# Sums, squares and Toeplitz copies of a hybrid decoder step: from GpSimd to VectorE and ScalarE

## The chip, the cores and the metric

The kernel runs on the 8 cores of one Trainium2 chip, as two dies of four cores (0 to 3, 4 to 7). Each core has its own sequence and runs the same program, without traffic between cores. The metric is the device time of the slowest core in microseconds. Some executions are in a slow state, in which the cores of one die show a clearly lower granted clock; they are set aside, and only fast runs are compared.

Even among fast runs there is one more disturbance. In some of them the granted TensorE clock of some cores is 0.8125 for a stretch, mostly of some 150 us.

Engines: PE is TensorE, DVE is VectorE, ACT is ScalarE, POOL is GpSimd. In the lines of the profile ARENA stands for the kernel's buffers in SBUF, and PS for those in PSUM, into which the matmuls write (`PS<-ARENA`). An eviction is an instruction that takes a product out of PSUM. Excerpts of the profile show picked lines, word for word; lines between them are left out.

## The reference, cut to what matters

Four layers; every core takes one prompt of 2048 rows and 16 samples of 8 rows, in two passes of 1024 and 1152 rows. Weights are shared.

```python
for i in range(4):
    z = rmsnorm(h, g_mix) @ w_in            # three head groups: short conv, chunk mixing, Conformer conv
    h = h + concat(rmsnorm(y_a), rmsnorm(y_b), rmsnorm(y_c)) @ w_out
    f = rmsnorm(h, g_ffn)
    h = h + (silu(f @ w_gate) * (f @ w_up)) @ w_down          # the channel mixer, most of the work
    h = h + sigmoid(rmsnorm(h, g_ple) @ w_ple_gate) * (p[i] @ w_ple_proj)
y = rmsnorm(h, g_final)
```

## The kernel before

The kernel records operations in a graph, and a list scheduler written in Python plans them when the program is built: it assumes a duration for each operation and gives each to an engine. The orders and the waits between engines are then fixed. An operation lists the engines that may take it, with durations in ns; the first is the preferred one.

```python
def d_tt(n, psum=False, half=True):                  # tensor_tensor on VectorE
    if psum:
        return n / 0.96 + 64
    return n / (1.92 if half else 0.96) + 76
def d_pool(n):                                       # the same on GpSimd
    return 1.95 * n + 200

def tt(out_f, a_f, b_f, alu, n, r, w, psum=False, half=True, pool=True, ...):
    engs = {"dve": d_tt(n, psum, half)}
    if pool and not psum:
        engs["pool"] = d_pool(n)
    return g.op(engs, lambda e: e.tensor_tensor(out_f(), a_f(), b_f(), alu), r=r, w=w,
                lock=() if psum else LK, name=name, horizon=horizon)
```

The scheduler knows that GpSimd and VectorE's SBUF operations exclude each other, but only in its own time: nothing in the program enforces it.

```python
if e == "dve" and "dve" in o.lock and pool_lock[0] > t + 1e-9:
    k += 1          # VectorE takes no locked operation while GpSimd is planned to run
    continue
if e == "pool" and not o.dma and dve_lock[0] > t + 1e-9:
    k += 1
    continue
```

The channel mixer uses a Strassen form with seven products. Its operand sums are made on the fly, for the weights (1024 elements a partition, 1408 for the down projection) and for the activations (a quarter of the tile, 256 or 288 elements; 1024 or 1152 for the normed input).

```python
def sums(s):                                         # weight sums of one slab
    tt(sv(0), q(2), q(3), ALU.add, n, ...)
    tt(sv(1), sv(0), q(0), ALU.subtract, n, ...)
    tt(q(2), q(0), q(2), ALU.subtract, n, ...)
    tt(sv(2), q(1), sv(1), ALU.subtract, n, ...)
# activation sums behind SwiGLU: four tt of n = 2 * Q = 256 or 288
# squares of the norms: engs = {"act": d_act(n), "pool": d_pool(n), "dve": d_tt(n, False, not f32src)}
# ... the rest is cut
```

Evictions of the products are also `tt`, with one operand in PSUM; those go to VectorE alone.

## Time and profile before

| kernel before | value | where |
|---|---|---|
| fast runs | 3307.03, 3309.75, 3309.78 us | times |
| PE, DVE, ACT, POOL busy | 91%, 73%, 53%, 42% | page, part 1 |
| PE waiting for VectorE's tensor_tensor | 239.2 us, 51.4 of it the start | list of waits |
| 128x1024 f16 sum on VectorE | 972 ns on average, 685 ns where no GpSimd arithmetic overlaps it | groups by shape; records sorted by overlap |

From the page of the kernel before (core 2, one of those that had a stretch at 0.8125): the span, busy time of each engine, the chain of work that ended last (followed back from the last instruction, at each step to what released it), and the costliest groups (line, engine, operation, shapes, count; then busy us, mean ns of one; then idle time before them and who ended most of it).

```profile
span 3316.4 us, 62751 instructions; the slowest of 8 cores (3292.8 to 3316.4 us)
PE 3024.5 (91%) x23511; PEld 2236.6 (67%) x23542; DVE 2422.7 (73%) x4834; ACT 1752.5 (53%) x3392; POOL 1379.3 (42%) x1160
...
PE 69%; DVE 15%; ACT 6%; issue 5%; DMA 4%; SPq 0%; DVEq 0%; ACTq 0%
PE PS L933 69%; DVE ARENA L915 12%; ACT ARENA L908 3%; DVE ARENA L920 2%; DMA ARENA<-g 1%; DMA g<-ARENA 1%; ACT L764 1%; DMA ARENA<-x 1%; ACT ARENA L962 1%; ACT ARENA L974 1%; DVE ARENA L1302 0%; ACT ARENA L1531 0%; DVE ARENA L975 0%; DVE ARENA L1244 0%; DVE ARENA L1218 0%
...
L933 PE MATMUL PS<-ARENA 128*128 128x288 f16 (+7 forms) x23511 | 3024.5, 292 | 280.5 <-DVE ARENA L915 239.2
L915 POOL TENSOR_TENSOR ARENA<-ARENA 128x256 f16<-128x256 f16 (+11 forms) x811 | 1157.1, 1435 | 1099.4 <-DVE ARENA L915 700.2
L915 DVE TENSOR_TENSOR ARENA<-ARENA 128x1024 f16<-128x1024 f16 (+10 forms) x1889 | 1199.4, 674 | 124.6 <-ACT ARENA L962 54.1
L915 DVE TENSOR_TENSOR ARENA<-ARENA,PS 128x256 f32<-128x256 f32 (+9 forms) x2016 | 865.6, 446 | 553.3 <-PE PS L933 508.6
```

TensorE is the bottleneck: it is busy 91% and has 69% of the chain. GpSimd isn't in the chain at all. Yet the two lines for `tensor_tensor` on VectorE differ strangely: the one with SBUF operands alone has a mean of 674 ns, the one that reads PSUM 446 ns.

The list of waits (waiting engine and line, what it waited for; total us, times, longest us) says what stalls TensorE.

```profile
PE PS L933 <- DVE ARENA L915: 239.2, 160, 51.4
...
DVE ARENA L915 <- POOL ARENA L915: 7.5, 16, 0.6
```

TensorE waits for VectorE, and hardly anybody waits for a sum of GpSimd: VectorE does so for 7.5 us. The groups by shape, same columns as above, show how uneven VectorE's sums are.

```profile
L915 POOL TENSOR_TENSOR ARENA<-ARENA 128x1024 f16<-128x1024 f16 x134 | 299.8, 2243 | 193.6 <-DVE ARENA L915 190.2 <-ACT ARENA L908 1.2
L915 DVE TENSOR_TENSOR ARENA<-ARENA 128x1024 f16<-128x1024 f16 x274 | 258.8, 972 | 6.1 <-PE PS L933 4.9 <-ACT ARENA L1595 0.9
L915 DVE TENSOR_TENSOR ARENA<-ARENA 128x576 f16<-128x576 f16 x247 | 162.4, 696 | 14.7 <-ACT ARENA L908 14.2
L915 DVE TENSOR_TENSOR ARENA<-ARENA 128x256 f16<-128x256 f16 x188 | 98.2, 561 | 7.3 <-POOL ARENA L915 7.0 <-PE PS L933 0.3
L915 DVE TENSOR_TENSOR ARENA<-ARENA,PS 128x288 f32<-128x288 f32 x616 | 273.1, 450 | 215.5 <-PE PS L933 198.0 <-ACT ARENA L908 12.3
```

A sum of 256 elements takes 561 ns on average, longer than an eviction of 288 from PSUM (450 ns). The mean hides two populations, sorted here by whether a GpSimd arithmetic instruction overlaps: 128x1024 takes 685 ns (median) alone and 1257 ns (mean) overlapped, 128x576 452 and 1205 ns, 128x256 280 and 930 ns. Evictions from PSUM don't change (453 and 450 ns). (From here on, an instruction counts as blocked when work of GpSimd other than DMA issue overlaps it and it takes over 100 ns more than the median of its shape without overlap; what it takes more is the blocked time.)

The timeline around the entry to a channel mixer (start us, length us, engine, line, what, count, idle time before and what ended it):

```profile
2165.77 2.18 DVE L915 TENSOR_TENSOR ARENA<-ARENA 128x576 bf16<-128x576 bf16 x1
2168.96 5.43 DVE L915 TENSOR_TENSOR ARENA<-ARENA 128x576 f16<-128x576 f16 x2
2169.87 4.20 POOL L915 TENSOR_TENSOR ARENA<-ARENA 128x1024 f16<-128x1024 f16 x2
2174.32 0.81 DVE L915 TENSOR_TENSOR ARENA<-ARENA,PS 128x288 f32<-128x288 f32 x2
2174.54 0.56 PE L933 MATMUL PS<-ARENA 128*128 128x288 f16 x2 [3.29 <-DVE ARENA L915]
```

Two VectorE sums of 576 elements, some 0.9 us of work when nothing overlaps, take 5.43 us, while GpSimd works 4.20 us on two weight sums. The PSUM evictions that stand behind them in VectorE's order come at 2174.32, and TensorE, which waits for VectorE, has idled 3.29 us.

### The profile page before, as it was taken

The page shows a single profiled execution, that of the slowest core. Times are in us where ns is not written, and L with a number is a line of the kernel's source. Part 1 is how long each engine was busy: PE and PEld are TensorE (multiplying, and loading weights), DVE is VectorE, ACT ScalarE, POOL GpSimd, SP SyncE. Part 2 cuts the span into 40 slices and gives each one's busy share as a digit, 9 for nine tenths or more (in the row PEclk, how much of TensorE's full clock was granted, in tenths as well). Part 3 has the DMA queues.
Part 4 walks back from the last instruction along what each step waited for, and adds up shares of the span by engine and source line. Part 5 has one row for each costly group of instructions (what it writes and reads, how often), then busy time and mean ns, then how long its engine had stood idle before and what let it go on. Part 6 is the DMA issues. An engine that isn't in the chain of part 4 may idle for free.

```text
span 3316.4 us, 62751 instructions; the slowest of 8 cores (3292.8 to 3316.4 us)
## 1 busy us (share of the span) xinstructions
PE 3024.5 (91%) x23511; PEld 2236.6 (67%) x23542; DVE 2422.7 (73%) x4834; ACT 1752.5 (53%) x3392; POOL 1379.3 (42%) x1160
## 2 busy tenths in 40 slices
PE   3799998899989998899888999989999899998997
PEld 1468854787448854787556777667776677766776
DVE  2677586986778676985768767687676876858768
ACT  2654267444564367444585526855267552675525
POOL 0255533564346543565225343253432525415342
PEclk9888999999989999999989999999999999999999
DMA  6532465345623565447823346432465323643233
GB/s 127 117 64 49 81 111 107 72 78 101 138 50 57 96 108 109 77 81 149 180 51 65 60 86 131 85 64 57 75 130 101 60 52 75 132 97 62 52 73 94
DMA packets 87364, 294.90 MB, mean 89 GB/s; under 512 B 40224, under 2 KB 44576, under 8 KB 62496
## 3 DMA queue, kind: packets, MB, share of 16 engines
q0 software_dynamic: 31104, 222.18, 37.9%
q1 hardware_dynamic: 55968, 68.72, 7.1%
q8 instruction: 196, 3.21, 0.4%
q14 instruction: 96, 0.79, 0.1%
HBM read 481.71 MB, written 32.77 MB: 155 GB/s over the span
## 4 chain that ended last, share of the span: by engine, by line
PE 69%; DVE 15%; ACT 6%; issue 5%; DMA 4%; SPq 0%; DVEq 0%; ACTq 0%
PE PS L933 69%; DVE ARENA L915 12%; ACT ARENA L908 3%; DVE ARENA L920 2%; DMA ARENA<-g 1%; DMA g<-ARENA 1%; ACT L764 1%; DMA ARENA<-x 1%; ACT ARENA L962 1%; ACT ARENA L974 1%; DVE ARENA L1302 0%; ACT ARENA L1531 0%; DVE ARENA L975 0%; DVE ARENA L1244 0%; DVE ARENA L1218 0%
## 5 line engine op out<-in xcount | busy, mean ns | idle before, releaser
L933 PE MATMUL PS<-ARENA 128*128 128x288 f16 (+7 forms) x23511 | 3024.5, 292 | 280.5 <-DVE ARENA L915 239.2
L933 PEld LDWEIGHTS PS<-ARENA 128*128 128x128 f16 (+2 forms) x23542 | 2236.6, 99 | 1067.9 <-issue 390.9
L915 POOL TENSOR_TENSOR ARENA<-ARENA 128x256 f16<-128x256 f16 (+11 forms) x811 | 1157.1, 1435 | 1099.4 <-DVE ARENA L915 700.2
L915 DVE TENSOR_TENSOR ARENA<-ARENA 128x1024 f16<-128x1024 f16 (+10 forms) x1889 | 1199.4, 674 | 124.6 <-ACT ARENA L962 54.1
L915 DVE TENSOR_TENSOR ARENA<-ARENA,PS 128x256 f32<-128x256 f32 (+9 forms) x2016 | 865.6, 446 | 553.3 <-PE PS L933 508.6
L908 ACT ACTIVATE ARENA<-PS 128x256 f32<-128x256 f32 (+5 forms) x1756 | 715.1, 419 | 824.8 <-PE PS L933 703.5
L962 ACT ACTIVATE ARENA<-ARENA 128x512 bf16<-128x512 f32 (+3 forms) x415 | 267.7, 656 | 576.2 <-DVE ARENA L915 527.6
L908 ACT ACTIVATE ARENA<-ARENA 128x768 f16<-128x768 f32 (+6 forms) x284 | 238.4, 849 | 56.8 <-DVE ARENA L915 49.8
L974 ACT ACTIVATE ARENA<-ARENA 128x512 f16<-128x512 f32 (+3 forms) x356 | 255.3, 739 | 17.4 <-PE PS L933 12.5
L896 POOL DMA_DIRECT2D ARENA<-wpair x152 | 88.4, 582 | 404.4 <-PE PS L933 193.5
L764 ACT ACT_TABLE_LOAD x139 | 178.3, 1283 | 2.2
L920 DVE SCALAR_TENSOR_TENSOR ARENA<-ARENA,PS 128x288 f32<-128x288 f16 (+1 forms) x192 | 95.7, 526 | 29.9 <-PE PS L933 14.5
L908 ACT ACTIVATE ARENA<-PS,ARENA 128x288 f16<-128x288 f32 (+3 forms) x174 | 88.5, 561 | 31.6 <-PE PS L933 30.6
L1403 POOL TENSOR_TENSOR ARENA<-ARENA 128x3 f32<-128x3 f32 (+1 forms) x24 | 21.7, 904 | 143.0 <-DVE ARENA L1401 143.0
L975 DVE TENSOR_SCALAR ARENA<-ARENA 128x576 f16<-128x576 f16 (+3 forms) x156 | 71.8, 480 | 1.6 <-PE PS L933 0.3
L963 DVE TENSOR_TENSOR ARENA<-ARENA 128x576 bf16<-128x576 f16 (+3 forms) x93 | 50.0, 549 | 29.3 <-ACT ARENA L908 25.8
L963 POOL TENSOR_TENSOR ARENA<-ARENA 128x512 bf16<-128x512 f32 (+2 forms) x36 | 42.0, 1166 | 60.9 <-DVE ARENA L915 52.1
L1302 DVE SCALAR_TENSOR_TENSOR ARENA<-ARENA,PS 128x288 f16<-128x288 f16 (+3 forms) x56 | 38.4, 695 | 30.0 <-PE PS L933 29.6
L920 DVE SCALAR_TENSOR_TENSOR ARENA<-PS,ARENA 128x512 f16<-128x512 f32 (+2 forms) x96 | 48.4, 547 | 14.9 <-PE PS L933 14.4
L1595 ACT ACTIVATE ARENA<-ARENA 128x128 f16<-128x128 f16 (+1 forms) x66 | 43.8, 734 | 13.1 <-DVE ARENA L915 12.6
L896 POOL DMA_DIRECT2D ARENA<-wdn x32 | 18.8, 588 | 74.7 <-PE PS L933 54.3
L1218 DVE TENSOR_TENSOR ARENA<-ARENA 128x640 f16<-128x640 f32 x52 | 45.5, 932 | 0.0
(38 smaller groups left out, 257.3 us busy)
## 6 DMA issues: line engine op xcount, KB each, us to landing
ARENA<-wpair POOLq DMA_DIRECT2D x152, 1024.0 KB, 9.4
ARENA<-wdn POOLq DMA_DIRECT2D x32, 1408.0 KB, 11.5
t<-ARENA SPq DMA_DIRECT2D x4, 2560.0 KB, 16.5
ARENA<-t SPq DMA_DIRECT2D x4, 2560.0 KB, 16.9
ARENA<-wv POOLq DMA_DIRECT2D x8, 768.0 KB, 15.8
ARENA<-x SPq DMA_DIRECT2D x16, 288.0 KB, 13.6
y<-ARENA SPq DMA_DIRECT2D x16, 288.0 KB, 2.3
ARENA<-x SPq DMA_DIRECT2D x16, 256.0 KB, 28.8
```

Of the source, the lines that this page charges most:

```text
L764: e.preload_act_table_set(tbl[i])
L896: return g.op({"pool": 900}, lambda e: e.dma_start(out=out_f(), in_=in_f()), r=r, w=w, dma=nb, name=name, horizon=horizon)
L908: return e.activation(out_f(), in_f(), func, scale=scale if isinstance(scale, float) else scale(), **kw)
L915: return g.op(engs, lambda e: e.tensor_tensor(out_f(), a_f(), b_f(), alu), r=r, w=w, lock=() if psum else LK, name=name, horizon=horizon)
L920: return e.scalar_tensor_tensor(out_f(), a_f(), s_f if isinstance(s_f, float) else s_f(), b_f(), op0, op1)
L933: lambda e: e.matmul(out_f(), l_f(), r_f(), start=start, stop=stop, skip_group_check=True),
L962: return e.activation(sq.ap(), a, AF.Square)
L963: return e.tensor_tensor(sq.ap(), a, a, ALU.mult)
L974: return e.activation(hg.ap(), a, AF.Identity, scale=vc(gcol(k)))
L975: return e.tensor_scalar(hg.ap(), a, vc(gcol(k)), None, ALU.mult)
L1218: return e.tensor_tensor(o, a, b, ALU.mult)
L1595: lambda e, t=t, k=k, i0=i0, o0=o0, m=m: (e.activation(t.ap()[:, o0:o0 + m], x.ap()[:, i0:i0 + m], AF.Identity, scale=vc(V0 + 32 + k * 3 + j))
```

## The change

The intent is to take GpSimd's arithmetic away where VectorE or ScalarE can do it. In the built programs, GpSimd loses 859 `tensor_tensor`, VectorE goes from 4836 to 5724 instructions, and ScalarE from 3258 to 3230. GpSimd keeps DMA issue, memsets, tiny copies, eight mask products and the powers. The plan is made anew, so the order of everything else moves too.

```diff
--- before.py
+++ after.py
@@ -803,6 +803,7 @@
 
 PRODS = (1, 2, 6, 5, 7, 3, 4)
 PDT = F16
+POOL_MAX = 0
 
 
 def d_tt(n, psum=False, half=True):
@@ -910,7 +911,7 @@
 
     def tt(out_f, a_f, b_f, alu, n, r, w, psum=False, half=True, pool=True, name="tt", urgent=False, horizon=None):
         engs = {"dve": d_tt(n, psum, half)}
-        if pool and not psum:
+        if pool and not psum and d_pool(n) < POOL_MAX:
             engs["pool"] = d_pool(n)
         return g.op(engs, lambda e: e.tensor_tensor(out_f(), a_f(), b_f(), alu), r=r, w=w,
                     lock=() if psum else LK, name=name, horizon=horizon)
@@ -954,7 +955,7 @@
         hgs = {}
         for i, k in enumerate(ks):
             sq = g.tile([n], BF16, "sq", top=True)
-            engs = {"act": d_act(n), "pool": d_pool(n), "dve": d_tt(n, False, not f32src)}
+            engs = {"act": d_act(n), "dve": d_tt(n, False, not f32src)}
 
             def fsq(e, sq=sq, k=k):
                 a = src(k)()
@@ -1216,7 +1217,7 @@
                     a = CST.ap()[:, 0:16].unsqueeze(1).unsqueeze(3).to_broadcast([128, 5, 16, 8])
                     b = TV.ap()[:, 5 * q:5 * q + 5, :].unsqueeze(2).to_broadcast([128, 5, 16, 8])
                     return e.tensor_tensor(o, a, b, ALU.mult)
-                g.op({"dve": d_tt(640, False, False), "pool": d_pool(640)}, ftz, r=[(CST, 0), (TV, 0)], w=[(TZ, q)], lock=LK, name="tz")
+                g.op({"dve": d_tt(640, False, False)}, ftz, r=[(CST, 0), (TV, 0)], w=[(TZ, q)], lock=LK, name="tz")
             hw_dma(lambda: sct[l], lambda: flat(TZ), [(TZ, range(16))], [(dtz, 0)], 128 * 20480, name="tzst")
         else:
             hw_dma(lambda: flat(TZ), lambda: sct[l], [(dtz, 0)], [(TZ, range(16))], 128 * 20480, name="tzld")
@@ -1530,7 +1531,7 @@
                         if hasattr(e, "activation"):
                             return e.activation(tv(sq), cv(j), AF.Square)
                         return e.tensor_tensor(tv(sq), cv(j), cv(j), ALU.mult)
-                    g.op({"act": d_act(nn), "dve": d_tt(nn), "pool": d_pool(nn)}, fsq, r=[(CC[j], u)], w=[(sq, 0)], lock=LK, name="lsq")
+                    g.op({"act": d_act(nn), "dve": d_tt(nn)}, fsq, r=[(CC[j], u)], w=[(sq, 0)], lock=LK, name="lsq")
 
                 def p2():
                     rb = g.tile([nn], F16, "lrb", top=True)
```

## The prediction

> What bounds the kernel now. The page of core 2 (span 3316.4 us, granted clock 0.965) has PE busy 91%, DVE 73%, ACT 53%, POOL 42%. In the chain of waits PE has 69% and DVE 15%; POOL has none. By the groups PE idles 280 us, and DVE line 915 ends 239 us of it (51 us of that is the start). TensorE bounds the kernel; what can be won is the some 190 us in which it waits for VectorE, plus the half-clock stretches after such gaps.
>
> Why VectorE is late. The same instruction has two lengths. Grouping DVE records by shape and by whether a POOL arithmetic instruction overlaps: 128x1024 f16 sums take 685 ns alone, 1257 ns on average when overlapped; 128x576 f16 452 and 1205; 128x256 f16 280 and 930. Sums with a PSUM operand don't change (128x288: 453 and 450). The Trainium skill (SBUF — State Buffer, "Who interferes with whom") says that a DVE instruction with two SBUF inputs and a GpSimd instruction that reads SBUF exclude each other, the second blocking fully; this trace agrees. Over all shapes DVE loses 370 us so. In the timeline at 2169 us two 128x576 sums on DVE take 5.43 us while POOL runs two 128x1024 sums (4.20 us), and PE then idles 3.29 us.
>
> What the change moves. The instruction order of both built programs: POOL loses 859 tensor_tensor; DVE goes from 4836 to 5724, ACT from 3258 to 3230. Removed: about 1120 us of POOL work. Added to DVE, at unblocked medians (134 x 685 ns, 56 x 884, 164 x 280, 132 x 301, about 170 x 453, about 160 x 420 and so on): about 420 us. Removed from DVE: 370 us of blocking. So DVE busy should stay nearly level, 2400 to 2500 us: what POOL did costs VectorE about what it already paid for it.
>
> How much is on the critical path. Walking back from each PE gap ended by DVE through the unbroken run of DVE work before it: of 194 us of such gaps, 104 us follow runs with blocking in them. Per layer the entry to the channel mixer (580-640 us, 2160-2220 us) has about 12 us of PE gaps, some 17 us of blocking, 35 us of POOL work that becomes about 12 us of DVE work: a net relief of 5 to 7 us. Times eight layers, 40 to 55 us. The Trainium skill (TensorE: Matmul & The Clock Gate, Part 1) says an idle PE falls to half clock; the clock records agree (3.4 to 6.8 us at 0.5 after the gaps at 592, 603 and 2176 us), so 10 to 20 us more. Gaps ended by ACT-bound norms, the conv's DMA round trips and the start stay.
>
> Predicted 3240 us (2.1% faster), 3195 to 3285; chances 0.52 faster, 0.46 within 2%, 0.02 slower.
>
> Signs. Right: 128x1024 f16 sums on DVE all near 685 ns; DVE busy about 2450 us; POOL under 200 us; PE idle down from 280 us by 50 or more; the gap at the mixer's entry down from 3.3 us to about 1. Wrong: DVE busy above 2600 us; PE idle unchanged with DVE at 95% at the same stages.
>
> What would make it wrong. The plan is rebuilt and may put sums before PSUM evictions, which opens new gaps; the gaps may be bound by norm chains on ACT, then the gain is under 1%; a denser PE may be granted less clock.

## More of the kernel before

Where experiments are compared closely I use the profiled run and take the mean span over the cores whose clock record has no stretch at 0.8125 ("undisturbed cores"). That is cores 4 to 7 for the kernel before (3296.4 us) and all eight for the kernel after (3114.8 us).

## The result, and the profile after

In the rounds of the first comparison the fast runs of the changed kernel took 3124.08 and 3127.17 us, those of before 3307.03, 3309.75 and 3309.78. The ratio is 0.9446, with a 95% interval from 0.9419 to 0.9474; a ratio is the mean time of one kernel's fast runs over that of the other's in the same rounds. So it is 5.5% faster.

The page of the kernel after (core 3; L916 and L934 are L915 and L933 moved by the added line):

```profile
span 3122.5 us, 62461 instructions; the slowest of 8 cores (3108.2 to 3122.5 us)
PE 2959.3 (95%) x23542; PEld 2224.7 (71%) x23542; DVE 2399.4 (77%) x5722; ACT 1730.0 (55%) x3364; POOL 161.1 (5%) x301
...
PE 87%; ACT 4%; DVE 4%; DMA 4%; issue 1%; SPq 0%; DVEq 0%; POOL 0%; ACTq 0%
PE PS L934 87%; ACT ARENA L909 2%; DVE ARENA L916 2%; DMA ARENA<-x 1%; DVE ARENA L921 1%; DMA ARENA<-g 1%; ACT L764 1%; ACT ARENA L963 1%; DMA g<-ARENA 1%; DMA y<-ARENA 0%; DVE ARENA L1219 0%; SPq L894 0%; DVE ARENA L1303 0%; ACT ARENA L1532 0%; ACT ARENA L975 0%
...
L934 PE MATMUL PS<-ARENA 128*128 128x288 f16 (+6 forms) x23542 | 2959.3, 289 | 151.7 <-DVE ARENA L916 132.1
L916 DVE TENSOR_TENSOR ARENA<-ARENA 128x1024 f16<-128x1024 f16 (+11 forms) x2700 | 1232.6, 489 | 123.4 <-ACT ARENA L963 61.2
L916 DVE TENSOR_TENSOR ARENA<-ARENA,PS 128x256 f32<-128x256 f32 (+9 forms) x2016 | 867.1, 445 | 412.5 <-PE PS L934 399.0
```

From its list of waits:

```profile
PE PS L934 <- DVE ARENA L916: 132.1, 52, 53.4
```

GpSimd's busy share falls from 42% to 5%, and VectorE's busy time falls too, from 2422.7 to 2399.4 us, although it has 888 instructions more. TensorE's idle time in the group falls from 280.5 to 151.7 us; its wait for VectorE from 239.2 to 132.1 us, of which 53.4 us is the start.

The groups by shape of the kernel after:

```profile
L916 DVE TENSOR_TENSOR ARENA<-ARENA 128x1024 f16<-128x1024 f16 x408 | 272.7, 683 | 8.1 <-PE PS L934 6.7 <-ACT ARENA L1596 0.9
L916 DVE TENSOR_TENSOR ARENA<-ARENA 128x576 f16<-128x576 f16 x320 | 133.2, 451 | 6.2 <-ACT ARENA L909 4.3 <-PE PS L934 0.9
L916 DVE TENSOR_TENSOR ARENA<-ARENA 128x256 f16<-128x256 f16 x352 | 88.5, 285 | 2.3
L916 DVE TENSOR_TENSOR ARENA<-ARENA,PS 128x288 f32<-128x288 f32 x616 | 276.7, 450 | 163.5 <-PE PS L934 159.1 <-ACT ARENA L909 0.3
```

The means are now the unblocked times: 683 ns for a sum of 1024, 285 ns for 256. On undisturbed cores VectorE's busy time less its blocked time rose by some 345 us, while its blocked time fell by 373: the moved work costs VectorE a little less than it used to lose.

The timeline at the same stage of the kernel after; the matmul that ended the 3.29 us gap stands at 14794 in its trace, where the records of 31 earlier matmuls are missing, and number 14825 of the complete trace here starts at 2039 us. First TensorE's line, then VectorE's:

```profile
2009.82 50.36 PE L934 MATMUL PS<-ARENA 128*128 128x288 f16 x408
...
2031.59 0.44 DVE L916 TENSOR_TENSOR ARENA<-ARENA,PS 128x288 f32<-128x288 f32 x1
2031.95 0.81 DVE L916 TENSOR_TENSOR ARENA<-ARENA 128x576 f16<-128x576 f16 x2
2032.69 0.44 DVE L916 TENSOR_TENSOR ARENA<-ARENA,PS 128x288 f32<-128x288 f32 x1
2033.05 0.81 DVE L916 TENSOR_TENSOR ARENA<-ARENA 128x576 f16<-128x576 f16 x2
2033.79 0.44 DVE L916 TENSOR_TENSOR ARENA<-ARENA,PS 128x288 f32<-128x288 f32 x1
```

TensorE runs 50.36 us there without a break. VectorE alternates short sums and evictions. The busy time in a stretch of 60 us at that stage, before and then after:

```profile
core 2: us, PE busy (x) PEld busy (x) DVE busy (x) ACT busy (x) POOL busy (x), PEclk, DMA share, GB/s
2160.00:2220.00 60.00, 50.37 (x382) 36.57 (x381) 54.52 (x94) 29.36 (x60) 33.52 (x24) 0.97 0.38 71
```

```profile
core 3: us, PE busy (x) PEld busy (x) DVE busy (x) ACT busy (x) POOL busy (x), PEclk, DMA share, GB/s
2010.00:2070.00 60.00, 59.94 (x490) 47.62 (x489) 58.08 (x141) 42.02 (x79) 1.58 (x3) 1.00 0.40 77
```

VectorE's busy share went up, from 54.52 to 58.08 of 60 us, and TensorE's from 50.37 to 59.94. But the two stretches don't hold the same work: TensorE ran 382 matmuls in the first and 490 in the second. For the same matmuls VectorE is busy less long than before; a table in the section on the prediction has the figures.

Where 181.6 us went (3296.4 to 3114.8, mean of undisturbed cores, from the traces):

| part of TensorE's time | before | after | gain |
|---|---|---|---|
| idle between matmuls | 230.1 | 96.9 | 133.2 |
| lost to half clock while it works | 56.7 | 32.7 | 24.0 |
| the rest of its working time | 2946.3 | 2921.5 | 24.8 |

The three gains sum to 182.0; the start and the end took 0.4 us more. The second row is half of the time that the clock record has at 0.5, outside the idle gaps. The third row is mostly the other part of the same stalls. The profile models the end of a matmul: for 288 columns it stands 286 ns after the start (median), while the next matmul mostly starts after 123 ns. So where TensorE stalls, the last matmul still counts as busy for a while. Outside half clock, 210 matmuls a core were followed by an idle gap before and 70 after; beyond the gap itself their successors were 34.6 and 11.8 us late in all, which is 22.8 of the 24.8 us.

### The profile page after: what moved, and what is told of

Same layout as the page of the kernel before. It is cut to its first block, busy times and chain, and to the rows that moved or that the text cites. A ratio compares the mean times of both kernels' runs of the same rounds, so it can differ in the third digit from the quotient of the medians.

```text
span 3122.5 us, 62461 instructions; the slowest of 8 cores (3108.2 to 3122.5 us)
## 1 busy us (share of the span) xinstructions
PE 2959.3 (95%) x23542; PEld 2224.7 (71%) x23542; DVE 2399.4 (77%) x5722; ACT 1730.0 (55%) x3364; POOL 161.1 (5%) x301
## 4 chain that ended last, share of the span: by engine, by line
PE 87%; ACT 4%; DVE 4%; DMA 4%; issue 1%; SPq 0%; DVEq 0%; POOL 0%; ACTq 0%
PE PS L934 87%; ACT ARENA L909 2%; DVE ARENA L916 2%; DMA ARENA<-x 1%; DVE ARENA L921 1%; DMA ARENA<-g 1%; ACT L764 1%; ACT ARENA L963 1%; DMA g<-ARENA 1%; DMA y<-ARENA 0%; DVE ARENA L1219 0%; SPq L894 0%; DVE ARENA L1303 0%; ACT ARENA L1532 0%; ACT ARENA L975 0%
## 5 line engine op out<-in xcount | busy, mean ns | idle before, releaser
L934 PE MATMUL PS<-ARENA 128*128 128x288 f16 (+6 forms) x23542 | 2959.3, 289 | 151.7 <-DVE ARENA L916 132.1
L934 PEld LDWEIGHTS PS<-ARENA 128*128 128x128 f16 (+2 forms) x23542 | 2224.7, 99 | 886.0 <-issue 217.8
L916 DVE TENSOR_TENSOR ARENA<-ARENA 128x1024 f16<-128x1024 f16 (+11 forms) x2700 | 1232.6, 489 | 123.4 <-ACT ARENA L963 61.2
L916 DVE TENSOR_TENSOR ARENA<-ARENA,PS 128x256 f32<-128x256 f32 (+9 forms) x2016 | 867.1, 445 | 412.5 <-PE PS L934 399.0
L963 ACT ACTIVATE ARENA<-ARENA 128x512 bf16<-128x512 f32 (+3 forms) x398 | 257.5, 655 | 539.4 <-DVE ARENA L916 484.3
L975 ACT ACTIVATE ARENA<-ARENA 128x512 f16<-128x512 f32 (+3 forms) x341 | 247.1, 741 | 5.8 <-DVE ARENA L916 4.5
L897 POOL DMA_DIRECT2D ARENA<-wpair x152 | 81.6, 539 | 1993.8 <-PE PS L934 1114.3
L964 DVE TENSOR_TENSOR ARENA<-ARENA 128x576 bf16<-128x576 f16 (+3 forms) x146 | 81.1, 563 | 21.6 <-ACT ARENA L909 20.7
L909 ACT ACTIVATE ARENA<-PS,ARENA 128x288 f16<-128x288 f32 (+2 forms) x174 | 89.3, 561 | 10.4 <-PE PS L934 6.6
L976 DVE TENSOR_SCALAR ARENA<-ARENA 128x512 f16<-128x512 f16 (+3 forms) x171 | 67.4, 415 | 1.5 <-PE PS L934 0.2
L1408 DVE TENSOR_SCALAR ARENA<-ARENA 128x384 f16<-128x384 f32 x68 | 29.4, 475 | 8.6 <-POOL ARENA L1404 7.0
```

The lines of the kernel that those rows point to most:

```text
L897: return g.op({"pool": 900}, lambda e: e.dma_start(out=out_f(), in_=in_f()), r=r, w=w, dma=nb, name=name, horizon=horizon)
L909: return e.activation(out_f(), in_f(), func, scale=scale if isinstance(scale, float) else scale(), **kw)
L934: lambda e: e.matmul(out_f(), l_f(), r_f(), start=start, stop=stop, skip_group_check=True),
L963: return e.activation(sq.ap(), a, AF.Square)
L964: return e.tensor_tensor(sq.ap(), a, a, ALU.mult)
L975: return e.activation(hg.ap(), a, AF.Identity, scale=vc(gcol(k)))
```

## The experiments

Three theories were set against each other. BLOCKING: GpSimd's reads lock VectorE's two-input sums out. SLOW RESULT: the sums take two to three times as long on GpSimd, and something waits for them. REPLAN: without GpSimd the planner finds a better order, whatever the hardware does. Later a question was added: does lost VectorE time count, or the length of a single stall?

All figures in this section without another label are mean spans of undisturbed cores.

### The plan of before, executed by VectorE

```diff
+    moved = [i for i in g.orders["pool"] if g.ops[i].prim != "pool" and not g.ops[i].dma and g.ops[i].name not in ("wm", "wms")]
+    for i in moved:
+        g.ops[i].eng = "dve"
+    gone = set(moved)
+    g.orders["pool"] = [i for i in g.orders["pool"] if i not in gone]
+    g.orders["dve"] = sorted(g.orders["dve"] + moved, key=lambda i: (g.ops[i].start, i))
```

> The plan of before is made as it was, GpSimd included; afterwards the 859 tensor_tensor that it gave to GpSimd are executed by VectorE, at the place in VectorE's order that their planned start gives. Same order, same allocation, no work on GpSimd. Theory BLOCKING (GpSimd's reads lock VectorE out and that makes TensorE wait) and theory SLOW RESULT (the sums take 2 to 3 times as long on GpSimd and something waits for them): most of the gain is there, 3120 to 3170 us, TensorE idle under 180 us. Theory REPLAN (with GpSimd gone the planner finds a better order): little of the gain, 3250 to 3310 us.

Ratio to before 0.952 (0.944 to 0.960); 3157.8 us on undisturbed cores. TensorE's idle time between matmuls is 125.0 us, against 230.1 in before. So 138.6 of the 181.6 us come with before's own plan, in which only the engine differs. The other 43.0 us come with the new plan. REPLAN alone is out, but it isn't nothing.

### The plan and engines of before, with instructions on GpSimd that read nothing

```diff
-        return g.op(engs, lambda e: e.tensor_tensor(out_f(), a_f(), b_f(), alu), ...)
+        return g.op(engs, lambda e: e.memset(out_f(), 0.01) if ON[0] == "pool" else e.tensor_tensor(...), ...)
```

(The squares got the same edit. The result is wrong on purpose.)

> Plan, order and engines of before, but every sum and square that GpSimd did is a memset of the same output on GpSimd (result wrong on purpose). It reads nothing, so two-input sums on VectorE should not be blocked, and it is probably shorter. BLOCKING or SLOW RESULT: 3110 to 3180 us. REPLAN: 3250 us or more, as the plan is before's.

Ratio 0.950 (0.945 to 0.954); 3145.6 us. By shape:

```profile
L917 POOL MEMSET ARENA<- 128x1024 f16 x134 | 126.7, 955 | 216.7 <-DVE ARENA L917 209.4 <-ACT ARENA L910 5.8
L917 DVE TENSOR_TENSOR ARENA<-ARENA 128x1024 f16<-128x1024 f16 x274 | 180.0, 684 | 6.1 <-PE PS L935 4.7 <-ACT ARENA L1599 1.1
```

The plan is before's and GpSimd still does each of these steps, in 955 ns instead of 2243 for 1024 elements. VectorE's sums are at 684 ns. This run alone doesn't part BLOCKING from SLOW RESULT, since memset is also shorter. Together with the last one it prices the added work: the same plan with the moved sums on VectorE has 294.6 us more VectorE busy time (2396.1 against 2101.5) and is 12.2 us longer, 0.04 us of total for a microsecond. (The memsets can cost something themselves, as a later run shows, so this price is rather low.)

### Sums that nobody uses, put back on GpSimd

To the kernel after, whose plan stays the same to the instruction, 946 sums were added on a private tile, one every 3.15 us of planned time.

```diff
+                if not isinstance(i, int):
+                    e.wait_ge(sems[self.eidx["dve"]], i.count)
+                    ins = e.tensor_tensor(JUNK[:, 0:512], JUNK[:, 512:1024], JUNK[:, 512:1024], ALU.add)
+                    ins._wait_ge(semj, nj)
+                    ins.then_inc(semj, 1)
```

(The rest of the edit is cut. `i` is then a filler that stands between GpSimd's own instructions, and the first wait paces it by VectorE's progress.)

> The kernel after, plan unchanged to the instruction, plus 946 tensor_tensor 128x512 f16 on GpSimd (about 1.14 us each, 1.08 ms in all) on a private tile that nobody uses, each let go by a VectorE semaphore so that they spread evenly. BLOCKING: VectorE's two-input sums get long again (128x1024 f16 mean well over 800 ns instead of 685), total 3170 to 3290 us. SLOW RESULT and REPLAN: nobody waits for these sums and the plan is the good one, so 3115 to 3140 us.

The twin has `e.memset(JUNK[:, 0:1024], 0.0)` in place of the sum:

> As junk_read, but each junk instruction is a GpSimd memset of 128x1024 f16, which writes and reads nothing. All theories: 3115 to 3140 us, VectorE's two-input sums at 685 ns. If it is as slow as junk_read, then GpSimd being busy at all costs (semaphores, DMA issue behind it), not its reads of SBUF.

The sums cost everything the change had won: ratio to before 1.013 (1.006 to 1.019), 3352.2 us, which is even above the range of BLOCKING. The memsets: ratio 0.948 (0.942 to 0.953), 3143.1 us. The groups by shape, first of the run with sums, then of the one with memsets:

```profile
L776 POOL TENSOR_TENSOR JUNK<-JUNK 128x512 f16<-128x512 f16 x946 | 1095.6, 1158 | 1947.7 <-DVE ARENA L935 1619.4 <-DVE ARENA L940 92.2 <-DVE ARENA L983 66.0
L935 DVE TENSOR_TENSOR ARENA<-ARENA 128x1024 f16<-128x1024 f16 x408 | 319.0, 796 | 5.6 <-PE PS L953 4.9
L935 DVE TENSOR_TENSOR ARENA<-ARENA 128x576 f16<-128x576 f16 x320 | 168.5, 560 | 2.1 <-ACT ARENA L928 1.1
L935 DVE TENSOR_TENSOR ARENA<-ARENA 128x256 f16<-128x256 f16 x352 | 139.8, 429 | 2.3
```

```profile
L776 POOL MEMSET JUNK<- 128x1024 f16 x946 | 908.0, 960 | 1929.2 <-DVE ARENA L935 1608.5 <-DVE ARENA L940 85.1 <-DVE ARENA L983 72.4
L935 DVE TENSOR_TENSOR ARENA<-ARENA 128x1024 f16<-128x1024 f16 x408 | 272.7, 683 | 7.2 <-PE PS L953 6.7
L935 DVE TENSOR_TENSOR ARENA<-ARENA 128x576 f16<-128x576 f16 x320 | 133.2, 450 | 5.7 <-ACT ARENA L928 4.1 <-PE PS L953 0.4
L935 DVE TENSOR_TENSOR ARENA<-ARENA 128x256 f16<-128x256 f16 x352 | 88.6, 285 | 2.3
```

GpSimd's arithmetic is busy 1.14 ms with the sums and 0.96 ms with the memsets (1.26 ms in before). With sums, VectorE's 128x256 sums go from 285 to 429 ns on average and VectorE loses 423 us; with memsets they stay at 285 ns. Nobody waits for this result and the plan is the good one, so this is BLOCKING, and it is shown: what harms is that GpSimd reads SBUF while VectorE wants two SBUF inputs. SLOW RESULT isn't needed for a loss of this size; in before itself it isn't isolated by a run, but there only 7.5 us of VectorE's waits were for a sum of GpSimd. The memsets still cost 28 us over the kernel after, more than any theory here expected. In their run VectorE loses 64 us, among others in its 128x1024 tensor_scalar, which takes 476 ns alone and 1031 ns overlapped. That part would fit the Trainium skill (SBUF — State Buffer, "Who interferes with whom"): a VectorE instruction in a two-port mode contends with any GpSimd instruction, a two-input one only with those that read. Whether these tensor_scalar ran in such a mode isn't shown by the profile.

### Lost VectorE time, or the length of a stall?

The same pace, but the fillers stand in VectorE's own order, right after the instruction that paced them.

```diff
+                if name == "dve" and i in paced:
+                    ins = e.tensor_tensor(JUNK[:, 0:768], JUNK[:, 768:1536], JUNK[:, 768:1536], ALU.add)
```

(The rest of the edit is cut.)

> The kernel after, plan unchanged to the instruction, plus 946 tensor_tensor 128x768 f16 on VectorE itself (550 ns each alone, some 470 ns back to back, so about 440 us in all), on a private tile that nobody uses, at the same even pace as the junk of junk_read. VectorE so loses as much time as the 425 us that GpSimd's reads took from it in junk_read, which cost 240 us. LOST TIME (what counts is how much VectorE time goes, in whatever pieces; my prediction's sum rested on this when it set added work against removed blocking): about as slow as junk_read, 3290 to 3370 us. LONG STALL (what counts is that one urgent instruction is held for 1 to 2 us; pieces of half a microsecond are absorbed): 3130 to 3200 us.

3271.2 us (ratio 0.986, 0.983 to 0.989), with 383.8 us more VectorE busy time than the kernel after: 156.4 us of total, 0.41 us for a microsecond. It falls below the range of LOST TIME and far above that of LONG STALL. Short pieces that ignore urgency do hurt.

Then GpSimd fillers of other lengths, the edit being the shape (1024 every 6.3 us, 256 every 1.78 us):

> As junk_read (the kernel after, same plan, unused sums on GpSimd at an even pace), but 476 sums of 128x1024 f16 (2.13 us each) in place of 946 of 128x512: GpSimd is as long busy, about 1.05 ms, in pieces of double length. So far a blocked microsecond cost 0.5 us of total in before (370 blocked, 180 lost) and 0.55 in junk_read (425 blocked, 235 lost), 0.8 in pool_big (240 blocked, 190 lost). LONG STALL: 0.7 us or more per blocked microsecond, total 3360 us or more. LOST TIME: 0.5 to 0.6 as in junk_read, whatever the length.

> As junk_long, but 1594 sums of 128x256 f16 (about 0.67 us each), again about 1.05 ms in all. LONG STALL: 0.4 us or less per blocked microsecond, total 3180 to 3270 us. LOST TIME: 0.5 to 0.6 per blocked microsecond.

| fillers on GpSimd | VectorE blocked, us | mean block, us | total over the kernel after, us | per blocked us |
|---|---|---|---|---|
| 1594 of 256 | 249.3 | 0.34 | 113.3 | 0.45 |
| 946 of 512 | 423.3 | 0.61 | 237.4 | 0.56 |
| 476 of 1024 | 503.6 | 1.31 | 309.0 | 0.61 |

(Total: span less 3114.8 us. The last row is of cores 2 and 3 alone, as the others had a stretch at 0.8125; its ratio to before, 1.047, includes those; that of the first row is 0.977, 0.971 to 0.983. The total of the middle row holds what GpSimd's fillers cost without reading: against its twin with memsets it is 209.1 us, for 359 us more of lost VectorE time, 0.58 for one.) Neither theory passes its own test cleanly: 0.61 isn't 0.7, and 0.45 isn't 0.5 to 0.6. The cost per blocked microsecond grows mildly with the length. What grows more is the blocked time itself, which doubles from short to long fillers, though GpSimd's arithmetic is busy no longer (1.19 ms with the short ones, 1.02 ms with the long).

### Which of the moved sums did the harm

The new parameter lets one part go back. First the small ones, the activation sums (`POOL_MAX = 800`; 287 of 256 or 288 elements. The text calls them "Toeplitz-like"; they are Strassen operand sums):

> The change, but sums of up to 288 elements (155 of 256 and 132 of 288: the Toeplitz-like T sums behind the channel mixer's activations, about 0.7 us each, 200 us in all) may still go to GpSimd. If the cost follows the blocked time at the rate of before (370 us blocked, 185 us of total), some 66 us are blocked and 3140 to 3180 us result. If only long GpSimd instructions hurt, 3115 to 3140 us.

3126.7 us, 11.9 over the kernel after; ratio 0.942 (0.939 to 0.945). VectorE is blocked 34.8 us. Small sums on GpSimd are nearly harmless: they block little, though the plan was made anew too, and this run doesn't part the two. The big ones (`if pool and not psum and d_pool(n) > 2100:`; 268 sums of 1024 to 1408):

> The change, but sums of 1024 elements and more (177 of 1024, 68 of 1408, 23 of 1152: mostly weight sums with slack, 2.1 to 2.9 us each, 630 us in all) may still go to GpSimd. If the cost follows the blocked time at the rate of before, some 200 us are blocked and 3200 to 3260 us result. If sums without a deadline can be put where they do no harm, as the planner intends, 3120 to 3160 us.

3312.1 us; ratio 0.998 (0.995 to 1.001). A third of the moved sums brings the whole loss back, more than either theory expected. To see whether its plan is simply bad, that plan was executed with those sums on VectorE, by the edit of the first experiment:

> The plan of pool_big (only sums of 1024 elements and more on GpSimd), with those 268 sums executed by VectorE at their planned place, as same_plan_dve does for before. pool_big took 3312 us a core, 197 us more than after, with 239 us of blocking. If the blocking makes that time: 3120 to 3170 us (the plan itself may be some 40 us worse, as the plan of before is). If pool_big's plan is simply bad: 3230 us or more.

3165.2 us: 146.9 us of pool_big's excess is GpSimd doing the sums, for 239.1 us of blocking in 147 stalls of 1.62 us on average (0.61 us per blocked microsecond), and 50.4 us is the plan. Its fast runs took 3193.12 to 3220.85 us (ratio 0.963, 0.952 to 0.973), and most cores in them show a mean granted clock of 0.96 to 0.98; in the profiled run cores 2 and 3 had a stretch at 0.8125.

The unchanged kernel after ran beside it:

> The kernel after, unchanged, for a comparison on one chip with big_plan_dve and with before: 3115 to 3130 us in fast runs, 0.94 to 0.95 of before.

Ratio 0.950 (0.939 to 0.962), fast runs 3143.97 to 3169.59 us: slower than expected, with stretches at 0.8125 on die 0 of the profiled run; its undisturbed cores 4 to 7 took 3115.0 us.

### An attempt to do better

The mask products and the tiny copies were taken from GpSimd too (`"pool"` left out of their engine lists).

> An attempt to beat the kernel after: the masks of W_s (eight products of 128x768, 1.6 to 1.9 us each) and the tiny copies leave GpSimd too; only DMA issue, memsets and the 24 powers stay. In the trace of after GpSimd still blocks 7.5 us of VectorE, near the channel mixer's entry. If every blocked microsecond counts 0.5 to 0.8: 4 to 6 us less, 3118 to 3122 us. If a re-made plan is worth more than that either way: 3110 to 3140 us.

Blocking falls from 7.6 us to none, and the time stays: 3114.9 against 3114.8 us; fast runs 3119.73 to 3133.34 us. No version beat the kernel after.

## Why the prediction was right or wrong

- **Bottleneck and cause: right.** TensorE bounds the kernel, and GpSimd's reads block VectorE. The pair of fillers, reading and not reading, shows it.
- **VectorE's load: right.** 2400 to 2500 us were predicted and 2399 measured, with all 128x1024 sums near 685 ns (683) and GpSimd under 200 us (161).
- **The critical path: wrong in size, and this is the step that failed.** The prediction took "some 17 us of blocking" per entry to the channel mixer against "35 us of POOL work that becomes about 12 us of DVE work: a net relief of 5 to 7 us", and so 40 to 55 us for eight entries and nothing elsewhere. TensorE's idle time fell by 133.2 us. The table below follows the same matmuls through four runs. The 17 us of blocking were right. But taking the blocking away (before to memsets, which also takes away any wait for a slow sum) shortened an entry by 11.0 us, and giving VectorE the moved sums (memsets to the same plan on VectorE) lengthened it by 0.4 us, although VectorE was busy 7.0 us longer. So the subtraction was false. With the new plan an entry is 13.6 us shorter, 109 us for the eight. The other 71 of the 180 us between the first and the last matmul came outside these entries, where the prediction counted nothing. Over the whole kernel, work that the planner places costs 0.04 us of total per microsecond (12.2 for 294.6 us), while a blocked microsecond cost 0.42 us in before (150.8 us between before and the memset run, with 380.4 less 17.1 us of blocking). The two can't be set off against each other. Why a planned microsecond is so cheap is argued, not isolated: the planner puts the sums behind urgent evictions, and VectorE's unplanned fillers, which ignore urgency, cost 0.41.
- **The bound that was in hand was ignored.** The walk back from TensorE's gaps had found 104 us that follow blocking, double the sum that was predicted. Of the 133.2 us that went, 117.9 were gaps ended by VectorE, 11.5 by a DMA and 1.3 by ScalarE.
- **Half clock: mechanism right, size a little small.** 10 to 20 us were predicted, 24.0 measured. (The three stretches that the prediction names took 3.4 us each in core 2's record.) The Trainium skill (TensorE: Matmul & The Clock Gate, Part 1) gives a half clock after idleness; this trace agrees, with fewer such stretches as the gaps went.
- **A term that was missing.** The part of each stall in which the last matmul still counts as busy gave most of 24.8 us.
- **Replanning was seen only as a risk.** It was a gain: 43.0 us between nearly the same sums on VectorE in before's plan and in the new one. (This cuts the same 181.6 us another way, and isn't added to the rows above.)

| one entry to the channel mixer, us | before | memsets on GpSimd | before's plan, sums on VectorE | after |
|---|---|---|---|---|
| length | 59.1 | 48.1 | 48.5 | 45.5 |
| VectorE busy | 54.0 | 38.2 | 45.2 | 44.1 |
| TensorE idle | 9.4 | 1.5 | 1.7 | 0.0 |

(Means over eight stretches, 402 matmuls each in the first pass and 380 in the second, placed by the prediction's windows, and over the undisturbed cores whose matmul records are complete: three before, six in each other run.)

The prediction's range ended at 3195 us; the fast runs are at 3124 to 3127.

## What to carry to other kernels

When an engine's mean instruction time is well above its own median, sort the records by what runs beside them before you believe the busy share: 374 blocked instructions of some 4800 carried most of the problem here. Work moved onto a busy engine isn't a cost by its busy time; ask whether the order lets urgent instructions pass first, and don't subtract it from stalls that nothing can pass. Long GpSimd instructions that read SBUF are the ones to move first: with 268 of them the kernel was as slow as with all 859, though 50.4 us of that were its plan.

## What the Trainium skill lacked or had wrong

- SBUF — State Buffer, "Who interferes with whom", has the block right (128x1024 f16: 685 ns free, 1257 overlapped; memsets leave two-input sums at 683 ns). It gives no measure of what a block costs the rest of a kernel. Here it was 0.42 to 0.61 us of total per blocked microsecond; in the timeline before, the evictions stand behind the blocked sums in VectorE's order.
- Perfetto Trace Analysis, "Optimizing Scalar/DVE Operations", says that offloading between VectorE and GpSimd "might not help". Here it did harm: 138.6 of 3296.4 us, with the plan held fixed.
- GPSIMD Engine Reference, 3.1, measures a `tensor_tensor` in fp32 (1.96 times slower on GpSimd). It has no such measurement in f16. For f16 sums of 1024 the ratio was 3.1 (2133 ns median against 685 ns).
- TensorE: Matmul & The Clock Gate, Part 1, says that with three busy cores a whole die goes to 13/16 clock and stays there while the load lasts, and advises to budget 1.95 GHz for all-core work. In the profile of the kernel after none of eight busy cores had a stretch at 0.8125 (mean granted clock 0.981 to 0.984). Some executions of the same kernel do show a whole die at a lower clock: in the slow run of 3574.43 us die 1 had 0.835 to 0.842 on average, die 0 0.981 to 0.983. So it came in some executions only. Where stretches occurred they covered about 150 to 160 us of 3300 (before, cores 0 to 3), at most 623 us (junk_long, core 5), and in the profile of big_plan_dve they took two cores of a die (2 and 3) and left the other two alone.
